# A sparse attention layer as a three-stage pipeline, with float32 up-projections and moved output weights

## The chip, the cores and the metric

The kernel runs on one core of a Trainium2 chip, as one program. The metric is the device time of one execution in microseconds; the table below gives the median of three. TensorE multiplies matrices, VectorE and ScalarE work elementwise on SBUF and PSUM, GpSimd (POOL in the profile) works on SBUF alone, SyncE (SP) issues most of the loads.

## The reference

256 tokens of width 1024 in float32 go through: a sparse attention layer, a feed-forward layer (width 2816), a gated scan layer, a second feed-forward layer, and a block of two mixers with a third feed-forward layer. The change is mainly in the attention layer:

```python
h = x @ w_in                      # 1024 -> 256 (c_q) + 128 (k) + 128 (v) + 128 (k_idx) + 8 (w_idx)
c_q = rms_norm(c_q, g_cq)
q = (c_q @ w_uq)                  # 256 -> 16 heads x 64
q_idx = (c_q @ w_iq)              # 256 -> 8 heads x 128
k_idx = layer_norm(k_idx, g_ik, b_ik)
# rope on q, k, q_idx, k_idx
score = einsum('bqh,bhqs->bqs', w_idx, relu(q_idx . k_idx))   # causal
_, sel = lax.top_k(score, 64)     # 64 keys for each query
p = softmax(q . k[sel] / 8)       # 2 key-value groups of 8 heads
out = (p @ v[sel]) @ w_o          # 1024 -> 1024
h = layer_norm(ALPHA * h + out)
```

The other layers are touched only where they take the root of a variance or mean square, and where the scan layer's constants are loaded.

## The kernel before, in words

The 256 tokens are two row tiles t = 0, 1 of 128 rows. Every weight matrix is streamed: `unit` (L183) loads up to 128x1024 elements into a `raw` tile (four buffers) from SP's queue, and `halves` (L173) makes two reduced float32 tiles of it, the high half `rhi` on ScalarE (L174) and the rest `rlo` on VectorE (L176) or, for the keys in `ON_POOL`, in pieces of 256 columns on GpSimd (L181). `rhi` and `rlo` have nine buffers each. `mm3` (L208) multiplies with three matmuls (L210 to L212), so a product is as good as float32.

The order of the attention layer is the string `DSA` (L1268), whose steps are written one after the other: x turns the input (`newT`), w loads weights, A and B are the input projections, r and f the angle tables, s.t.n the scores of half n of the indexer heads (`score`, L480), q.t.n the queries (`query`, L518), p the top-k (`pick`, L504: eight rounds of maximum and replacement), a.t.g the attention of head group g (`attend`, L523), o.n.t half n of the output projection (L579), n the layer norm, z the transposition for the next layer. Both s and q call `up` (L471): a projection from 256 to 512 columns, a copy to SBUF, `rope` (L369, three elementwise instructions on 128x128) and four transpositions.

The text order is a priority. A planner at build time puts the instructions of each engine into an order by its own estimate of when their inputs are there; on the chip each engine then takes its instructions in that order. `later` (L107) binds the instructions traced within it behind the last one traced so far on VectorE, ScalarE and TensorE.

In `attend` a block is 512 columns of logits: four heads for t = 0 (four blocks in all) and two heads for t = 1 (eight). It multiplies the mask by a large negative diagonal (L534), adds the logits by native float32 matmuls (L538), and calls `softmaxT` (L592): maximum, exponentials and their sums on ScalarE (L599), reciprocal, scaling on ScalarE (L228), four transpositions and a copy on VectorE (L224); then the values (L547). The next block is traced after that. The output weights `dsa_o` are in `ON_POOL`; they are loaded and split where o first asks for them, at the end of the string, but their instructions depend on nothing else.

Roots are taken on GpSimd: `rstd` (L254) scales and adds epsilon (L257) and raises to -0.5 (L258); `rstd_halves` (L891) takes two such additions (L897, L898) and the power (L899). `hgrn_consts` (L696), traced beside the first feed-forward layer, loads three constant blocks into `raw` tiles.

Of the kernel before, what the change touches and what calls it, by code (L numbers as in the profile page):

```python
# [19 lines left out]
P = 128  # L20
D = 1024
# [66 lines left out]
class Net:  # L88
# [6 lines left out]
    def __init__(self, tc, ins, consts, out, ctx):  # L95
# [8 lines left out]
        self.carried = None  # L104

    @contextlib.contextmanager
    def later(self):  # L107
# [5 lines left out]
        engines = {self.nc.vector.engine, self.nc.scalar.engine, self.nc.tensor.engine}  # L113
# [155 lines left out]
    def sumsq(self, s, src, dst, junk):  # L269
        self.nc.scalar.activation(junk[:, : src.shape[-1]], src, AF.Square, accum_out=dst)  # L270

    def ln_residual(self, t, ys, g, b):
# [6 lines left out]
        r = self.rstd(t, mv[:, 1:2], 1, 1.0, LN_EPS)  # L279
# [8 lines left out]
    def norm_heads(self, s, o, heads, d, dst):  # L288
# [3 lines left out]
        nc.scalar.activation(sq, o, AF.Square)  # L292
        ss = self.sm(s, heads, name="ss")
        nc.vector.tensor_reduce(ss, sq, AX.X, ALU.add)
        r = self.rstd(s, ss, heads, 1.0 / d, RMS_EPS)
# [89 lines left out]
    def setup(self):  # L385
# [4 lines left out]
        a = self.bank("y1")  # L390
        for i in range(WARM):
            nc.tensor.matmul(a, warm[:, 0:P], warm[:, 512:1024], start=i == 0, stop=i == WARM - 1)
# [28 lines left out]
    def dsa(self, dst):  # L421
# [8 lines left out]
        w = {}  # L430
# [4 lines left out]
        def inA(t):  # L435
# [4 lines left out]
            self.sumsq(t, a[:, :256], ss, n)  # L440
            r = self.rstd(t, ss, 1, 1.0 / 256, RMS_EPS)
# [14 lines left out]
        def inB(t):  # L456
# [3 lines left out]
            r = self.rstd(t, mv[:, 1:2], 1, 1.0, LN_EPS)  # L460
# [62 lines left out]
        def attend(t, g):  # L523
# [6 lines left out]
            if True:  # L530
                oT = self.bank("dO%d" % t, (P, 4, P), name="oT")
                for i, h0 in enumerate(range(0, 8, per)):
                    L = self.bank("dL%d" % t, (P, per, nk), name="L")
                    nc.tensor.matmul(  # L534
                        L, self.negI, nsel[:, None, :nk].to_broadcast([P, per, nk]), start=True, stop=False
                    )
                    for j in range(0, per, 2):
                        nc.tensor.matmul(  # L538
                            L[:, j : j + 2, :], qT[t][:, g * 4 + (h0 + j) // 2, :], kT[:, g, :, :nk],
                            start=False, stop=j == per - 2,  # L540
                        )
                    pT = self.softmaxT(t, L, per, nk, "d%d" % (i % 2))
                    for j in range(per):
                        h = h0 + j
                        e = (h % 2) * 64
                        for kc in range(t + 1):
                            nc.tensor.matmul(  # L547
                                oT[e : e + 64, h // 2, :], vs[kc][:, g * 64 : (g + 1) * 64],
                                pT[:, j * (t + 1) + kc, :], start=kc == 0, stop=kc == t,
                            )  # L550
                b = slice(g * 4, g * 4 + 4)
                self.halves(OT[t][0][:, b, :], OT[t][1][:, b, :], oT)

        def load(key):
# [6 lines left out]
            else:  # L561
                w[key] = self.group({"iq": w_iq, "uq": w_uq}[key], 0, 1024, 256, "dsa_" + key)
# [4 lines left out]
        def angles(s):  # L567
# [7 lines left out]
            "w": load, "x": turned, "r": angles, "f": lambda: w["r"](), "A": inA, "B": inB, "s": score, "p": pick, "q": query, "a": attend,  # L575
# [3 lines left out]
        def out(n, t):  # L579
            if not rows:  # L580
                rows.extend(self.ln_rows(0, 0))
            if n not in groups:
                groups[n] = self.group(w_o, n * 512, 512, D, "dsa_o")
# [7 lines left out]

    def softmaxT(self, s, L, per, nk, site):  # L592

# [7 lines left out]
        for j in range(per):  # L601
            self.scaled(p[:, j, :], p[:, j, :], rc[:, j : j + 1], "p" + site)
        pT = self.w2(s, (P, 4, P), name="pT")
        self.copy(pT, self.blocksT(self.cols(p.rearrange("p h k -> p (h k)"), 0, 4), site[0] + "P%d" % s), "pT" + site)
        return pT


    def ffn(self, i, HT, wg, wu, wd, finish, turn=None, aside=None):
# [41 lines left out]
        def beside(i):  # L650
            with self.later():
                aside[i]()
# [43 lines left out]
    def hgrn_consts(self):  # L696

        nc, ins, mx = self.nc, self.ins, self.bound
        raw = lambda: self.tile("raw", (P, 1024), F32, "raw")
        sel = self.load(raw()[0:8, :], self.const("sel", 8)).rearrange("p (a b) -> p a b", a=8)  # L700
# [8 lines left out]
        nc.vector.tensor_copy(lev, self.load(raw(), self.const("lev")))  # L709
        msk = self.w1(1, (P, 6, 32), mybir.dt.uint8, name="msk")  # L710
        o, n = OFF["msk"]
        both = self.load(raw()[:, : n + P + 64], self.consts[:, o : o + n + P + 64])
# [178 lines left out]
    def rstd_halves(self, t, halves):  # L891

        nc = self.nc
        s2, v, r = self.sm(t, 2, name="s2"), self.sm(t, 2, name="rv"), self.sm(t, 1, name="rs")
# [490 lines left out]
```

## Time and profile before

| | us |
|---|---|
| median of 3 runs | 1159.03 |
| lowest, highest | 1153.61, 1160.45 |
| profiled execution | 1154.16 |
| its span, first to last instruction | 1152.4 |
| TensorE busy in the span | 1106.6 (96%) |
| VectorE, ScalarE, GpSimd busy | 697.3, 583.9, 224.3 |

A profile is one execution. Busy time of TensorE is modelled to the end of each matmul, so two matmuls in a row overlap by some 0.15 us in the listing; the distance of their starts is what a matmul costs in a row of them. In a listing a row has start, duration, engine, line, operation, out<-in, count, and in brackets the idle time before it and what ended that. The attention layer ends near 120 us.

### The profile page before, as it was taken

To read this page: it belongs to the slowest core of one execution; us is meant where nothing else is said; L and a number is where in the kernel's file an instruction comes from. 1 tells how busy PE (TensorE), PEld (TensorE's weight loads), DVE (VectorE), ACT (ScalarE), POOL (GpSimd) and SP (SyncE) were. 2 spreads that over 40 slices of the span, in tenths; PEclk is the share of its full clock that TensorE was granted. 3 is DMA by queue.
4 is the path that set the end of the run, shared out by engine and by line. 5 is a ranking of instruction groups with operands and counts; after the bars stand their busy time and mean duration, and the time that the engine had idled before them with its cause. 6 is when DMAs were issued, how large, how long until landed. Compare 5 with 4: busy or idle time off the path is not lost.

```text
span 1152.4 us, 15343 instructions
## 1 busy us (share of the span) xinstructions
PE 1106.6 (96%) x5724; PEld 903.0 (78%) x5724; DVE 697.3 (61%) x1061; ACT 583.9 (51%) x832; POOL 224.3 (19%) x336
## 2 busy tenths in 40 slices
PE   8779999999999999999999999999999999999997
PEld 6546888878888777788888887887788878888886
DVE  6986755535566677875545486446655547454542
ACT  5656455525467466444444346763546456453441
POOL 2800620000432223200000022534100181000000
PEclk9989999999999899999999999999999999999999
DMA  8420756547445342365656545663554446566541
GB/s 250 159 85 5 243 166 229 182 119 255 146 146 173 103 145 77 119 214 180 218 183 192 175 131 174 207 159 102 164 192 146 146 146 225 174 222 202 171 140 37
DMA packets 98458, 187.33 MB, mean 163 GB/s; under 512 B 9400, under 2 KB 26952, under 8 KB 98384
## 3 DMA queue, kind: packets, MB, share of 16 engines
q1 hardware_dynamic: 94816, 176.28, 48.1%
q0 software_dynamic: 2864, 9.45, 2.5%
q8 instruction: 45, 0.74, 0.3%
q10 hardware_dynamic: 704, 0.62, 0.2%
q14 instruction: 29, 0.24, 0.1%
HBM read 185.28 MB, written 1.05 MB: 162 GB/s over the span
## 4 chain that ended last, share of the span: by engine, by line
PE 81%; DVE 8%; POOL 4%; DMA 3%; issue 2%; ACT 2%; SPq 0%; POOLq 0%; DVEq 0%; ACTq 0%
PE a L210 15%; PE a L211 15%; PE a L212 15%; PE y L211 8%; PE y L210 8%; PE y L212 8%; PE t L236 3%; POOL rlo L181 2%; DVE rlo L176 1%; PE lv L830 1%; DMA raw<-in_ffn_w_up_dram 1%; DMA raw<-in_ffn_w_gate_dram 1%; DVE m L381 1%; ACT rhi L174 1%; PE L L538 1%
## 5 line engine op out<-in xcount | busy, mean ns | idle before, releaser
L176 DVE TENSOR_TENSOR rlo<-raw,rhi 128x1024 fp32r<-128x1024 f32 (+4 forms) x306 | 370.2, 1215 | 216.3 <-ACT rhi L174 204.8
L174 ACT ACTIVATE rhi<-raw 128x1024 fp32r<-128x1024 f32 (+3 forms) x338 | 352.7, 1047 | 242.8 <-PE y L212 75.5
L210 PE MATMUL a<-rhi,xh 128*128 128x512 f32 (+4 forms) x840 | 318.6, 379 | 3.4 <-ACT sil L625 1.8
L211 PE MATMUL a<-rlo,xh 128*128 128x512 f32 (+4 forms) x840 | 316.7, 377 | 0.2 <-DVE rlo L176 0.2
L212 PE MATMUL a<-rhi,xl 128*128 128x512 f32 (+4 forms) x840 | 315.4, 376 | 0.0
L210 PEld LDWEIGHTS a<-rhi,xh 128*128 128x128 f32 x840 | 158.7, 189 | 32.1 <-ACT xh L174 2.0
L211 PEld LDWEIGHTS a<-rlo,xh 128*128 128x128 f32 x840 | 158.8, 189 | 27.8 <-DVE rlo L176 0.6
L212 PEld LDWEIGHTS a<-rhi,xl 128*128 128x128 f32 x840 | 158.8, 189 | 27.4
L181 POOL TENSOR_TENSOR rlo<-raw,rhi 128x256 fp32r<-128x256 f32 x128 | 99.2, 811 | 179.8 <-ACT rhi L174 179.7
L210 PE MATMUL y<-rhi,hth 128*128 128x512 f32 x264 | 104.7, 396 | 0.5 <-ACT hth L174 0.5
L212 PE MATMUL y<-rhi,htl 128*128 128x512 f32 x264 | 103.2, 391 | 0.0
L211 PE MATMUL y<-rlo,hth 128*128 128x512 f32 x264 | 102.9, 390 | 0.0
L210 PE MATMUL y<-rhi,xh 128*128 128x512 f32 (+2 forms) x152 | 59.1, 390 | 3.1 <-ACT rhi L174 3.1
L257 POOL TENSOR_SCALAR rv<-mv 128x1 f32<-128x1 f32 x10 | 7.2, 716 | 272.0 <-DVE mv L266 271.8
L211 PE MATMUL y<-rlo,xh 128*128 128x512 f32 (+2 forms) x152 | 59.0, 388 | 1.0 <-POOL rlo L181 0.6
L212 PE MATMUL y<-rhi,xl 128*128 128x512 f32 (+2 forms) x152 | 58.6, 387 | 0.0
L174 ACT ACTIVATE hth<-t 128x512 fp32r<-128x512 f32 (+1 forms) x36 | 20.1, 558 | 75.6 <-PE t L236 75.6
L210 PEld LDWEIGHTS y<-rhi,hth 128*128 128x128 f32 x264 | 49.6, 188 | 10.7 <-ACT hth L174 1.1
L212 PEld LDWEIGHTS y<-rhi,htl 128*128 128x128 f32 x264 | 49.5, 188 | 10.6
L211 PEld LDWEIGHTS y<-rlo,hth 128*128 128x128 f32 x264 | 49.6, 188 | 9.7
L631 DVE TENSOR_TENSOR sil<-a,sil 128x512 f32<-128x512 f32 (+1 forms) x36 | 23.2, 643 | 51.1 <-PE a L212 51.0
L625 ACT ACTIVATE sil<-a 128x512 f32<-128x512 f32 (+1 forms) x36 | 20.2, 561 | 58.9 <-PE a L212 58.8
(412 smaller groups left out, 1435.0 us busy)
## 6 DMA issues: line engine op xcount, KB each, us to landing
raw<-in_ffn_w_gate_dram SPq DMA_DIRECT2D x44, 512.0 KB, 4.7
raw<-in_ffn_w_up_dram SPq DMA_DIRECT2D x44, 512.0 KB, 4.7
raw<-in_ffn_w_down_dram SPq DMA_DIRECT2D x44, 512.0 KB, 4.6
raw<-in_hgrn_w_in_dram SPq DMA_DIRECT2D x32, 512.0 KB, 4.5
raw<-in_w_in_dram SPq DMA_DIRECT2D x24, 512.0 KB, 4.4
raw<-in_w_ffn_gate_dram SPq DMA_DIRECT2D x22, 512.0 KB, 4.3
raw<-in_w_ffn_up_dram SPq DMA_DIRECT2D x22, 512.0 KB, 4.6
raw<-in_w_ffn_down_dram SPq DMA_DIRECT2D x22, 512.0 KB, 4.5
```

The lines of the kernel that those rows point to most:

```text
L174: self.nc.scalar.activation(hi, src, AF.Copy)
L176: self.nc.vector.tensor_sub(lo, src, hi.bitcast(F32))
L181: eng.tensor_sub(lo[:, c], src[:, c], hi[:, c].bitcast(F32))
L210: mm(out, xh, wh, start=start, stop=False)
L211: mm(out, xh, wl, start=False, stop=False)
L212: mm(out, xl, wh, start=False, stop=stop)
L236: self.nc.tensor.transpose(tp[:, j, :], b, self.ident)
L381: e2.tensor_tensor(m2, v[:, :, ::-1, :], s[:, None, :, :].to_broadcast(sh), ALU.mult)
L538: nc.tensor.matmul(L[:, j : j + 2, :], qT[t][:, g * 4 + (h0 + j) // 2, :], kT[:, g, :, :nk], start=False, stop=j == per - 2,)
L625: nc.scalar.activation(sil[ci, t][:, :cn], a[:, :cn], AF.Silu)
L631: nc.vector.tensor_mul(sil[ci, t][:, :cn], a[:, :cn], sil[ci, t][:, :cn])
L830: nc.tensor.matmul(lv[64 * c : 64 * c + 64, l - l0, j, :32], y, late, start=True, stop=True)
```

## The change

It does six things.

1. The up-projections use native float32 matmuls: `whole` loads a 128x1024 block of `w_iq` or `w_uq` straight into an `rhi` or `rlo` buffer, `proj4` multiplies once, and `c_q` is no longer split.
2. The attention is a pipeline of three stages, `flow`: with the logits and softmax of one block the transpositions of the block before and the values of the one before that are traced. The mask matmul comes last in a block.
3. The output weights are loaded in two steps `wo.0` and `wo.1`; their ScalarE and GpSimd instructions are bound behind the last ones traced so far, and the first step puts one small GpSimd copy ahead that reads the last roped tile.
4. The order string is another one: queries and scores of both row tiles come ahead of the first attention step.
5. The roots have their scale folded into the square, their epsilon added on VectorE, and one GpSimd instruction left; two places in the attention keep the old form (`rstd_aside`).
6. Thirteen dummy matmuls stand after the second input tile's transposition, and the scan constants are loaded into tiles of the `w4` pool.

```diff
-    def later(self):
+    def later(self, *engines):
...
-        engines = {self.nc.vector.engine, self.nc.scalar.engine, self.nc.tensor.engine}
+        engines = {e.engine for e in engines}
...
+    def whole(self, w, K):
+        res = []
+        for k in range(K // P):
+            raw = self.tile(("rhi", "rlo")[k % 2], (P, 1024), F32, "whole")
+            self.nc.sync.dma_start(raw, w[k * P : (k + 1) * P, :])
+            res.append(raw)
+        return res
+
+    def proj4(self, out, xT, grp, sl):
+        n = len(grp)
+        for k, w in enumerate(grp):
+            self.nc.tensor.matmul(out, xT[:, k, :], w[:, sl], start=k == 0, stop=k == n - 1)
...
-    def rstd(self, s, src, n, scale, eps):
+    def rstd_aside(self, s, src, n, scale, eps):
         v = self.sm(s, n, name="rv")
+        self.nc.gpsimd.tensor_scalar(v, src, scale, eps, ALU.mult, ALU.add)
+        return self.root(s, v, n)
+
+    def root(self, s, v, n):
         r = self.sm(s, n, name="rs")
-        self.nc.gpsimd.tensor_scalar(v, src, scale, eps, ALU.mult, ALU.add)
         self.nc.gpsimd.tensor_tensor(r, v, self.nhalf[:, :n], ALU.pow)
         return r
+
+    def rstd(self, s, src, n, eps):
+        self.nc.vector.tensor_scalar(src, src, eps, None, ALU.add)
+        return self.root(s, src, n)
...
-            c = self.xt("cq")
-            cq[t] = (c[:, 0:2, :], c[:, 2:4, :])
-            self.splitT(n, cq[t][0], cq[t][1], 2, T[t])
+            cq[t] = self.tile("xt", (P, 2, P), F32, "cq")
+            nc.scalar.activation(cq[t], self.blocksT(self.cols(n, 0, 2), T[t]), AF.Copy)
...
-            self.proj(a, cq[t], grp, slice(n * 512, (n + 1) * 512))
-            s = self.w2(t, name="up")
+            self.proj4(a, cq[t], grp, slice(n * 512, (n + 1) * 512))
+            s = turned_last[0] = self.w2(t, name="up")
...
+            for i, h0 in enumerate(range(0, 8, per)):
+                self.flow(
+                    lambda h0=h0, i=i: logits(h0, i),
+                    lambda p, i=i: self.probsT(t, p, "d%d" % (i % 2)),
+                    lambda pT, h0=h0: values(h0, pT),
+                )
...
+        def load_out(n):
+            if n == 0:
+                nc.gpsimd.tensor_copy(self.sm(1, 1, name="gate"), turned_last[0][:, 0:1])
+            with self.later(nc.gpsimd, nc.scalar):
+                groups[n] = self.group(w_o, n * 512, 512, D, "dsa_o")
...
+    def flow(self, *stages):
+        if stages:
+            self.under.insert(0, [stages[0](), list(stages[1:])])
+            for block in self.under[1:]:
+                block[0] = block[1].pop(0)(block[0])
+        else:
+            for block in reversed(self.under):
+                while block[1]:
+                    block[0] = block[1].pop(0)(block[0])
+        self.under = [block for block in self.under if block[1]]
...
     def hgrn_consts(self):
-        raw = lambda: self.tile("raw", (P, 1024), F32, "raw")
-        sel = self.load(raw()[0:8, :], self.const("sel", 8)).rearrange("p (a b) -> p a b", a=8)
+        stage = [self.w4(name="stage") for _ in range(3)]
+        sel = self.load(stage[0][0:8, :], self.const("sel", 8)).rearrange("p (a b) -> p a b", a=8)
...
     def rstd_halves(self, t, halves):
-            self.sumsq(t, halves[n], s2[:, n : n + 1], self.w2(t, dt=BF16, name="sq"))
-        nc.gpsimd.tensor_scalar(v[:, 0:1], s2[:, 0:1], 1.0 / D, RMS_EPS, ALU.mult, ALU.add)
-        nc.gpsimd.tensor_scalar(v[:, 1:2], s2[:, 1:2], 1.0 / D, v[:, 0:1], ALU.mult, ALU.add)
-        nc.gpsimd.tensor_tensor(r, v[:, 1:2], self.nhalf[:, :1], ALU.pow)
-        return r
+            self.meansq(halves[n], s2[:, n : n + 1], self.w2(t, dt=BF16, name="sq"), D)
+        nc.vector.tensor_scalar(v, s2[:, 0:1], RMS_EPS, s2[:, 1:2], ALU.add, ALU.add)
+        return self.root(t, v, 1)
...
-WARM = 10
+WARM, WARM_X = 10, 13
...
 DSA = (
-    "x.0 X.1 x.1 w.A w.A2 r.0 f w.iq A.0 w.B B.0 s.0.0 A.1 B.1 w.uq s.1.0 s.0.1 q.1.0 q.0.0 p.0 s.1.1 q.0.1 a.0.0 "
-    "q.1.1 p.1 a.0.1 a.1.0 a.1.1 o.0.0 o.1.0 n.0 o.0.1 z.0 o.1.1 n.1 r.1"
+    "x.0 X.1 x.1 W w.A w.A2 r.0 f w.iq A.0 w.B B.0 s.0.0 A.1 B.1 w.uq s.1.0 s.0.1 s.1.1 q.0.0 q.0.1 q.1.0 p.0 q.1.1 "
+    "a.0.0 wo.0 p.1 a.0.1 a.1.0 wo.1 o.0.0 a.1.1 o.1.0 n.0 F o.0.1 z.0 o.1.1 n.1 r.1"
 )
```

In the order string W is the dummy matmuls and F ends the pipeline, so that the blocks still under way are finished.

## Rows read from the trace of the kernel before

**Rows 1.** Busy time by stretch: stretch, length, PE, PEld, DVE, ACT, POOL, clock, DMA, GB/s.
```profile
10.00:30.00 20.00, 19.18 (x112) 17.88 (x112) 17.32 (x55) 12.41 (x23) 3.89 (x7) 0.91 0.82 263
30.00:62.00 32.00, 21.25 (x108) 15.41 (x107) 30.55 (x74) 20.32 (x32) 25.40 (x36) 0.95 0.53 176
62.00:81.00 19.00, 14.55 (x75) 9.74 (x75) 16.68 (x50) 11.77 (x50) 0.00 (x0) 0.90 0.15 51
81.00:120.00 39.00, 39.00 (x223) 26.74 (x222) 26.36 (x46) 22.67 (x60) 1.31 (x2) 1.00 0.11 29
```

**Rows 2.** What TensorE waited for over the span: us in total, times, longest.
```profile
PE t L236 <- DVE up L382: 5.5, 2, 4.0
PE t L236 <- DVE h L910: 3.3, 3, 1.5
```

**Rows 3.** VectorE's groups from 27 to 62.5 us: count, busy us, mean ns, idle before.
```profile
L381 DVE TENSOR_TENSOR m<-up,sin 128x128 f32<-128x128 f32 x7 | 7.4, 1064 | 0.0
L380 DVE TENSOR_TENSOR m<-up,cos 128x128 f32<-128x128 f32 x7 | 4.0, 577 | 0.0
L499 DVE SCALAR_TENSOR_TENSOR keep<-rl,wi,keep 128x128 f32<-128x128 f32 x7 | 3.7, 532 | 0.5 <-ACT rl L494 0.4
L382 DVE TENSOR_TENSOR up<-m,m 128x128 f32<-128x128 f32 x7 | 3.5, 503 | 0.1
```

**Rows 4.** The order of time on VectorE and GpSimd, 45 to 60 us.
```profile
45.86 0.68 DVE L224 COPY qiT<-t 128x512 f32<-128x512 f32 x1
...
47.45 0.28 DVE L381 TENSOR_TENSOR m<-up,sin 128x128 f32<-128x128 f32 x1
...
54.67 5.54 POOL L181 TENSOR_TENSOR rlo<-raw,rhi 128x256 fp32r<-128x256 f32 x8
54.69 4.94 DVE L381 TENSOR_TENSOR m<-up,sin 128x128 f32<-128x128 f32 x1
```

**Rows 5.** Groups of the weight split, 0 to 170 us.
```profile
L174 ACT ACTIVATE rhi<-raw 128x1024 fp32r<-128x1024 f32 x35 | 37.0, 1059 | 23.6 <-PE a L212 9.8 <-DMA raw<-in_ffn_w_up_dram 4.5 <-PE y L212 4.4
L176 DVE TENSOR_TENSOR rlo<-raw,rhi 128x1024 fp32r<-128x1024 f32 x26 | 31.6, 1222 | 14.8 <-ACT rhi L174 14.0
L181 POOL TENSOR_TENSOR rlo<-raw,rhi 128x256 fp32r<-128x256 f32 x32 | 23.6, 769 | 5.3 <-ACT rhi L174 5.3
```

**Rows 6.** TensorE in the order of time: an up-projection, then a native float32 product.
```profile
31.57 0.40 PE L210 MATMUL y<-rhi,cq 128*128 128x512 f32 x1
31.81 0.40 PE L211 MATMUL y<-rlo,cq 128*128 128x512 f32 x1
...
81.01 1.02 PE L538 MATMUL L<-kT,qT 128*128 128x512 f32 x2
81.87 0.38 PE L236 MATMUL t<-ident,p 128*128 128x128 f32 x2
```

**Rows 7.** TensorE at the start, in the order of time.
```profile
1.73 3.68 PE L392 MATMUL y<-warm 128*128 128x512 bf16 x10 [1.73 <-POOL warm L389]
...
10.22 0.62 PE L210 MATMUL y<-rhi,xh 128*128 128x384 f32 x2 [3.07 <-ACT rhi L174]
```

**Rows 8.** The first logits and the first product of the feed-forward layer.
```profile
63.16 1.91 PE L538 MATMUL L<-kT,qT 128*128 128x256 f32 x4
...
120.06 0.39 PE L210 MATMUL a<-rhi,xh 128*128 128x512 f32 x1
```

**Rows 9.** Loads and TensorE's gaps in the first feed-forward layer, in the order of time.
```profile
234.52 25.61 SPq L188 DMA_DIRECT2D raw<-in_ffn_w_gate_dram  x6
...
242.99 0.74 PE L236 MATMUL t<-ident,sil 128*128 128x128 f32 x4 [2.05 <-DVE sil L631]
...
277.77 0.39 PE L210 MATMUL a<-rhi,xh 128*128 128x256 f32 x1 [1.79 <-ACT sil L625]
```

**Rows 10.** Busy time by stretch around those gaps, columns as in rows 1.
```profile
240.00:245.00 5.00, 2.95 (x13) 2.16 (x12) 2.44 (x3) 1.66 (x2) 0.00 (x0) 0.84 0.28 75
245.00:250.00 5.00, 5.00 (x20) 4.03 (x19) 2.00 (x3) 1.06 (x1) 0.00 (x0) 0.82 0.16 42
```

More of the change, by code (lines that the diff above doesn't have):

```diff
@@ L267, in meanvar, with meansq @@
         return mv
-    def sumsq(self, s, src, dst, junk):
-        self.nc.scalar.activation(junk[:, : src.shape[-1]], src, AF.Square, accum_out=dst)
+    def meansq(self, src, dst, junk, n):
+        self.nc.scalar.activation(junk[:, : src.shape[-1]], src, AF.Square, scale=n ** -0.5, accum_out=dst)
     def ln_residual(self, t, ys, g, b):
@@ L389, in setup, with keep_warm @@
         nc.gpsimd.memset(warm, 0.0)
-        a = self.bank("y1")
-        for i in range(WARM):
-            nc.tensor.matmul(a, warm[:, 0:P], warm[:, 512:1024], start=i == 0, stop=i == WARM - 1)
+        def keep_warm(count):
+            a = self.bank("a")
+            for i in range(count):
+                nc.tensor.matmul(a, warm[:, 0:P], warm[:, 512:1024], start=i == 0, stop=i == count - 1)
+        self.keep_warm = keep_warm
+        keep_warm(WARM)
         self.X = [self.cp.tile([P, D], F32, name=f"x{t}") for t in range(2)]
@@ L529, in attend, with logits @@
                 OT[t] = (self.xt("oh"), self.xt("ol"))
[L530 to L533, printed above, removed]
+            oT = []
+            def logits(h0, i):
+                L = self.bank("dL%d" % t, (P, per, nk), name="L")
+                for j in range(0, per, 2):
                     nc.tensor.matmul(
-                        L, self.negI, nsel[:, None, :nk].to_broadcast([P, per, nk]), start=True, stop=False
-                    )
-                    for j in range(0, per, 2):
+                        L[:, j : j + 2, :], qT[t][:, g * 4 + (h0 + j) // 2, :], kT[:, g, :, :nk],
+                        start=j == 0, stop=False,
+                    )
+                nc.tensor.matmul(
+                    L, self.negI, nsel[:, None, :nk].to_broadcast([P, per, nk]), start=False, stop=True
+                )
+                return self.softmax(t, L, per, nk, "d%d" % (i % 2))
@@ L538, in attend, with values @@
+            def values(h0, pT):
+                if not oT:
+                    oT.append(self.bank("dO%d" % t, (P, 4, P), name="oT"))
+                for j in range(per):
+                    h = h0 + j
+                    e = (h % 2) * 64
+                    for kc in range(t + 1):
                         nc.tensor.matmul(
-                            L[:, j : j + 2, :], qT[t][:, g * 4 + (h0 + j) // 2, :], kT[:, g, :, :nk],
-                            start=False, stop=j == per - 2,
-                        )
@@ L542, in attend @@
[L542 to L550, printed above, removed]
@@ L551, in attend @@
-                b = slice(g * 4, g * 4 + 4)
-                self.halves(OT[t][0][:, b, :], OT[t][1][:, b, :], oT)
+                            oT[0][e : e + 64, h // 2, :], vs[kc][:, g * 64 : (g + 1) * 64],
+                            pT[:, j * (t + 1) + kc, :], start=kc == 0, stop=kc == t,
+                        )
+                if h0 + per == 8:
+                    b = slice(g * 4, g * 4 + 4)
+                    self.halves(OT[t][0][:, b, :], OT[t][1][:, b, :], oT[0])
+            for i, h0 in enumerate(range(0, 8, per)):
[3 more added lines that the diff above has]
+                    lambda pT, h0=h0: values(h0, pT),
+                )
@@ L561, in load @@
             else:
-                w[key] = self.group({"iq": w_iq, "uq": w_uq}[key], 0, 1024, 256, "dsa_" + key)
+                w[key] = self.whole({"iq": w_iq, "uq": w_uq}[key], 256)
+        def load_out(n):
[3 more added lines that the diff above has]
+                groups[n] = self.group(w_o, n * 512, 512, D, "dsa_o")
         def turned(t):
@@ L590, in dsa, with softmax @@
         self.run(DSA, {**steps, "o": out, "n": close, "z": self.turner(dst)})
-    def softmaxT(self, s, L, per, nk, site):
+    def flow(self, *stages):
[8 more added lines that the diff above has]
+        self.under = [block for block in self.under if block[1]]
+    def softmax(self, s, L, per, nk, site):
         nc = self.nc
@@ L605, in softmaxT @@
         return pT
+    def softmaxT(self, s, L, per, nk, site):
+        return self.probsT(s, self.softmax(s, L, per, nk, site), site)
     def ffn(self, i, HT, wg, wu, wd, finish, turn=None, aside=None):
@@ L650, in beside @@
         def beside(i):
-            with self.later():
+            with self.later(nc.vector, nc.scalar, nc.tensor):
                 aside[i]()
```

31 lines of the change are left out of this document (16 added, 15 removed).

## The prediction

> **What bounds the kernel now.** First view: busy time by stretch of the attention layer, which ends at 120 us [rows 1]. Up to 62 us VectorE is the busiest engine (17.3 of 20 us, then 30.6 of 32) while TensorE has gaps (21.3 of 32); from 81 to 120 us TensorE has none (39.0 of 39). So the layer has two halves: one set by VectorE, one by TensorE. Behind it the feed-forward layers keep TensorE full, so what this layer saves stays saved. Second view: what TensorE waited for over the whole span [rows 2]. The longest entry is the transposition of up-projected rows waiting for rope (5.5 us); the 3.3 us for `h` lie at the two layer ends where an RMS norm follows.
>
> Third view: VectorE's groups from 27 to 62 us [rows 3]. Three rope instructions on one 128x128 shape average 1064, 577 and 503 ns. Fourth view, the order of time [rows 4]: the same instruction takes 0.28 us at 47.45, while GpSimd idles, and 4.94 us at 54.69, where it starts 0.02 us behind a GpSimd run that lasts 5.54 us. That run is the low half of the output weights. A copy out of PSUM at 45.86, beside an earlier such run, took 0.68 us, no longer than elsewhere. So VectorE's elementwise work between two SBUF tiles is held up by GpSimd, and this sits on the path.
>
> **The change, part by part.** The sum is made against the profiled execution, 1154.2 us; its span is 1152.4, so 1.8 us lie around it. The median of the runs shown, 1159.0, is 4.9 us above it.
>
> *Output weights moved.* The 32 GpSimd pieces of 769 ns [rows 5] (24.6 us) now start behind the last rope; their 8 conversions on ScalarE follow the softmax work given so far. Rope gets its clean 0.28 us: 7 x (1.064 + 0.577 + 0.503 - 3 x 0.28) = 9.1 us of VectorE time off the path [rows 3, 4]. Score and key-rope instructions gain too; I leave them out as reserve. SP's queue keeps the eight loads in their place but holds the four raw tiles longer: the first feed-forward loads queue behind the second half. They need about the time TensorE spends in the last output projections, so I cost this at nothing; if that cover fails it is the first rival.
>
> *Native float32 up-projections.* Gone are four splits of 128x1024: 4 x 1.059 us of ScalarE and 4 x 1.222 = 4.9 us of VectorE [rows 5]; the VectorE part counts. The price is TensorE's: today six matmuls per projection, 0.24 us apart from 31.57 to 31.81, so 1.4 us; a native 128x512 product shows as two records that hold the engine from 81.01 to 81.87, 0.86 us [rows 6], so two per projection are 1.7 us. Eight projections cost 8 x 0.3 = 2.4 us more, beside VectorE as long as that is the bound. The small splits of `cq` go as well; their gain is under 1 us and not counted.
>
> *Dummy matmuls before the first projection.* TensorE waits 3.07 us before 10.22 and its first 128x384 products come about 0.31 us apart; ten dummies took 3.68 us [rows 7]. Thirteen take up to 4.8 us at that pace, 1.7 us more than the gap. Against that stands a higher clock sooner. Between -1.7 and +2 us; I take 0, since the split weights arrive one by one there and set the pace either way.
>
> *Order and pipeline.* Logits of the first block start at 63.16, the first feed-forward product at 120.06 [rows 8]. New start of the logits, by VectorE: 63.2 - 9.1 - 4.9, plus what now comes ahead of it (one rope 0.84, four score additions at about 0.53 [rows 3]: 3.0), gives 52. By TensorE: 10.2 plus the busy time of 10 to 62 us, 19.2 + 21.3, gives 50.7, plus seven of the eight dearer projections, 2.1: 53 with no idle at all, less what its first products ran at a lowered clock (mean 0.91 over 20 us [rows 1], so 1.8 us): 51. I take 52. From there to the feed-forward start: TensorE owes 14.6 + 39.0 = 53.6 us [rows 1], so 105.6. ScalarE owes 11.8 + 22.7 = 34.4 us [rows 1] and 8 x 1.06 = 8.5 for the output weights, and needs some 2.5 us before its first exponential; that is 97.4, and then the second half of one projection and one whole one, (12 + 24) x 0.24 = 8.6 [rows 6], so 106.0. Both engines allow 106 against 120: **14 us** saved. Today each block waits for its own softmax, transposition and copy; the three stages let TensorE take the logits of the next block meanwhile, which is what makes 53.6 us of work fit in 54. Without that overlap, 5 us of gaps as today between 62 and 81 (19 - 14.6 [rows 1]) come back: 9 us saved. With the reserve above and a clean pipeline: 20. The mask matmul placed last lets the logits begin before the top-k has ended: worth about 1 us, inside this.
>
> *Scan constants in their own tiles.* SP's queue needs 25.6 us for six gate loads from 234.5, because three of four raw tiles hold constants; TensorE then waits 2.05 and 1.79 us [rows 9] and runs at a mean clock of 0.84 and 0.82 of full for 10 us [rows 10], which is 5 x (0.16 + 0.18) = 1.7 us lost. Together 5.5 us; the new tiles come from a pool that the attention layer has left. I take **5**; bounds 0 (no tile free in time) and 5.5.
>
> *Norm roots.* One GpSimd instruction of each root becomes a VectorE one or goes. Most of these chains lie beside matmuls of the other row tile. What TensorE shows of them is the 3.3 us for `h` [rows 2]; the chain keeps its power on GpSimd, so I take **2**, between -0.5 (VectorE places its short instruction behind a long one) and 4.
>
> Sum: 14 + 5 + 2 = 21, so 1154.2 - 21 = 1133 for the profiled execution. Since that run was low among the three, I set the median 2 us higher: **1135 us**. What is late next is TensorE itself, over almost all of the span.
>
> **A rule against a row.** The copy at 45.86 shows no delay beside GpSimd [rows 4]. The Trainium skill (SBUF — State Buffer, section "Who interferes with whom") says that VectorE and GpSimd share one port pair under an exclusive lock, taken by two-SBUF-input instructions and by copies in a two-port mode. By its first half the moved GpSimd work finds only the one mask comparison per row tile to block, so the sum stands; by its second half the twelve probability copies would be exposed, and that is the slower rival below. For a source in PSUM the row speaks for the first.
>
> **Rivals.**
> 1. *The gain is given back in the attention.* The second half of the output weights may convert only behind the first group's softmax of row tile 1; its four units need 1.06 + 4 x 4 x 0.77 = 13.4 us [rows 5], and 24 products (24 x 0.24 = 5.8 us) of row tile 1 follow. If that softmax ends at 92 instead of about 80, the feed-forward starts at 92 + 13.4 + 6 x 0.24 + 5.8 = 113, or its own weights are late by as much. For it: GpSimd's and SP's queues are in order. Against: ScalarE had 7 us of idle time in the 19 from 62 to 81 [rows 1], so the softmax can come sooner. Attention saves 7 instead of 14, with the rest 14: 1142 (median scale).
> 2. *The constants don't help*, because the stream there is slow for another reason or the new tiles come free late. For it: six loads spread over 25.6 us [rows 9] would also fit a slow memory. Against: the feed-forward layers before and after run the same stream with TensorE full. 1140.
> 3. *Slower: the hold-up travels with GpSimd's work.* Place: the twelve blocks' reductions and copies and the top-k of row tile 1, which now run beside the 24.6 us on GpSimd. Price: a hold like that at 54.69, 4.94 us [rows 4], once per unit, on six of the eight: 29.6 us. The feed-forward would start at 106 + 29.6 = 136, 16 later than now; less 7 from the other parts, and 2 for the scale: 1165. It decides from 21 us of such holds. Against it is the copy at 45.86; in the rows only instructions with two SBUF inputs suffer.
>
> **How the numbers follow.** Forecast 0.62 (its own range 1127 to 1141), first rival 0.18, second 0.12, third 0.05, the rest for a gain above the forecast's range. A measurement of this kernel can tell about 1% from no change, here 1147.4. The first rival reaches beyond that with about a third of its weight (the pipeline failing too), the second with a small part: faster 0.83, same 0.12, slower 0.05. The range takes in every bound of the parts on the good side, 1154 - 20 - 5.5 - 4 = 1124.5, and rivals 1 and 2 together, 1147, on the other: 1124 to 1149.
>
> **What would show it.** Right: rope on 128x128 near 0.28 us each; first logits near 52 us; first feed-forward product near 106; GpSimd's pieces all behind the last rope; no TensorE wait between 234 and 280 us and the clock full there; the native products as two records of 0.43 us. Wrong: feed-forward product after 112 us with TensorE idle between 60 and 100 (rival 1); SP still taking 25 us for six loads (rival 2); VectorE instructions of several microseconds beside GpSimd in the attention (rival 3). If TensorE is full from 12 us on and the layer still ends late, the native products were too dear.

## The result: 0.6% faster, and the attention layer no sooner done

| | before | changed |
|---|---|---|
| median of 14 runs each, side by side, us | 1154.31 | 1147.62 |
| ratio, 95% interval | | 0.9941 (0.9919 to 0.9964) |
| span of the profiled execution, us | 1152.4 | 1147.8 |
| first logits, us | 63.16 | 53.90 |
| first feed-forward product, us | 120.06 | 122.88 |

The gain is 6.7 us where 21 were forecast, and less than the 1% that the prediction took as the bound of what can be told from no change. The logits come 9.3 us sooner, as forecast within 2 us, and the attention layer ends 2.8 us later. What was gained was gained behind it. TensorE in the changed kernel, in order of time: a native projection, the first logits, the first mask, a later wait, the first feed-forward product (columns as in [rows 6]; here and below, L is a line of the kernel that was run, so the numbers differ from those of the kernel before).

```profile
49.13 1.88 PE L222 MATMUL y<-whole,cq 128*128 128x512 f32 x4
...
53.90 1.46 PE L565 MATMUL L<-kT,qT 128*128 128x256 f32 x6
...
58.28 0.59 PE L569 MATMUL L<-keep,negI 128*128 128x512 bf16 x2 [1.78 <-DVE keep L546]
...
102.81 0.67 PE L581 MATMUL oT<-pT,keep 128*64 128x128 f32 x8 [2.66 <-DVE pT L240]
...
122.88 0.39 PE L226 MATMUL a<-rhi,xh 128*128 128x512 f32 x1
```

The same stretch by busy time answers to [rows 1] (first 30 to 54 us, then from the first logits on):

```profile
30.00:54.00 24.00, 23.77 (x110) 14.71 (x109) 16.93 (x62) 10.38 (x19) 1.31 (x3) 1.00 0.06 22
...
53.90:58.00 4.10, 2.52 (x14) 1.74 (x13) 4.05 (x22) 2.68 (x4) 0.73 (x2) 1.00 0.20 52
58.00:76.00 18.00, 12.64 (x44) 6.56 (x44) 10.70 (x32) 13.76 (x50) 7.53 (x11) 0.72 0.19 55
76.00:99.80 23.80, 23.80 (x138) 14.94 (x136) 14.00 (x25) 18.77 (x52) 13.26 (x21) 1.00 0.36 108
99.80:108.00 8.20, 5.54 (x25) 4.18 (x24) 4.38 (x6) 2.72 (x8) 1.27 (x2) 0.79 0.60 188
108.00:122.88 14.88, 14.88 (x81) 11.64 (x81) 13.40 (x19) 7.39 (x9) 1.00 (x1) 1.00 0.33 92
```

Read PE (third figure) and the clock (eighth, the counts in brackets left aside) together. From 30 to 54 us TensorE is idle for 0.2 us and VectorE for 7.1: TensorE has become the bound there. After the logits, busy time times clock is an estimate of work done: 2.5 + 9.1 + 23.8 + 4.4 + 14.9 = 54.7 us of work in 69.0 us. So 14.3 us are lost, 8.9 of them from 58 to 76 and 3.8 from 99.8 to 108. The same estimate for the kernel before gives 52.3 us of work in 56.9, so 4.6 lost.

The first loss lies ahead of the first output product. The output projection begins with `oh`, the attended rows of the first head group, which ScalarE copies out of PSUM (`oT`). Before, then changed:

```profile
75.81 0.60 ACT L174 ACTIVATE oh<-oT 128x512 fp32r<-128x512 f32 x1 [0.56 <-PE oT L547]
76.45 0.50 PE L210 MATMUL y<-rhi,oh 128*128 128x512 f32 x1 [0.70 <-ACT oh L174]
```

```profile
67.35 3.88 ACT L175 ACTIVATE rhi<-raw 128x1024 fp32r<-128x1024 f32 x4
...
70.85 0.66 PE L581 MATMUL oT<-pT,keep 128*64 128x128 f32 x8
...
75.41 0.59 ACT L175 ACTIVATE oh<-oT 128x512 fp32r<-128x512 f32 x1
...
76.56 0.59 PE L226 MATMUL y<-rhi,oh 128*128 128x512 f32 x1
```

The first output product comes at 76.56 us, as late as before (76.45), though the logits began 9.3 us sooner: that lead is all used up here. Before, `oh` was copied 0.05 us behind its last product; now it is copied 3.9 us behind it (75.41 against 71.51), when ScalarE has done the exponentials of the third and fourth blocks, and four conversions of output weights stand ahead of those. From the first output product to the feed-forward layer it takes 46.3 us instead of 43.6.

The second loss lies in that last stretch and comes from VectorE and GpSimd (answers to [rows 4]):

```profile
90.01 11.06 POOL L182 TENSOR_TENSOR rlo<-raw,rhi 128x256 fp32r<-128x256 f32 x16 [10.54 <-ACT rhi L175]
...
97.79 4.36 DVE L177 TENSOR_TENSOR rlo<-raw,rhi 128x1024 fp32r<-128x1024 f32 x1
```

The low half of a feed-forward weight, 1.22 us elsewhere, takes 4.36 beside GpSimd's second run; the copy `pT` behind it is what TensorE waits for until 102.81. The hold of [rows 4] has moved from rope to here.

In the first feed-forward layer the gaps of [rows 9] and the lower clock of [rows 10] are gone,

```profile
230.00:280.00 50.00, 50.00 (x254) 42.18 (x253) 25.09 (x26) 24.24 (x28) 0.00 (x0) 1.00 0.55 180
```

and the waits for `h` in [rows 2] fall from 3.3 to 1.8 us:

```profile
PE t L252 <- DVE h L977: 1.8, 3, 0.7
```

### The profile page after: what moved, and what is told of

It is laid out like the page before. It is cut to its first block, busy times and chain, and to the rows that moved or that the text cites. A ratio compares the mean times of both kernels' runs of the same rounds, so it can differ in the third digit from the quotient of the medians.

```text
span 1147.8 us, 15285 instructions
## 1 busy us (share of the span) xinstructions
PE 1114.7 (97%) x5721; PEld 902.3 (79%) x5721; DVE 686.3 (60%) x1083; ACT 580.5 (51%) x828; POOL 204.4 (18%) x301
## 5 line engine op out<-in xcount | busy, mean ns | idle before, releaser
L175 ACT ACTIVATE rhi<-raw 128x1024 fp32r<-128x1024 f32 (+4 forms) x334 | 347.9, 1047 | 230.1 <-PE y L228 79.6
L278 POOL TENSOR_TENSOR rs<-mv,nhalf 128x1 f32<-128x1 f32 x8 | 8.0, 996 | 241.8 <-DVE mv L283 241.8
```

Source lines behind the costliest of these rows:

```text
L175: self.nc.scalar.activation(hi, src, AF.Copy)
```

## The experiments

Each profile starts a little differently (the first projection at 9.7 to 11.5 us), so "layer" below is the time from the first projection's product to the first feed-forward product. The three kernels with the attention layer of before show its scatter: 109.8, 111.9 and 109.5 us. "Hold" is the longest VectorE instruction that was held up beside GpSimd from 27 to 122 us; "output" is the first output product.

| run | first logits | output | hold | layer | ratio to before, 95% interval |
|---|---|---|---|---|---|
| before | 63.16 | 76.45 | 4.94 rope | 109.8 |  |
| changed | 53.90 | 76.56 | 4.36 | 112.3 | 0.9941 (0.9919 to 0.9964) |
| e1 constants and roots alone | 65.11 | 78.41 | 4.94 rope | 111.9 | 0.9944 (0.9926 to 0.9962) |
| e12 constants alone | 63.42 | 76.72 | 4.96 rope | 109.5 | 0.9975 (0.9961 to 0.9990) |
| e2 second half's low parts on VectorE | 53.76 | 77.34 | none | 109.4 | 0.9941 (0.9916 to 0.9966) |
| e3 top-k early | 53.69 | 75.51 | 1.62 | 108.0 | 0.9918 (0.9893 to 0.9943) |
| e4 ScalarE untied | 53.68 | 77.00 | none | 107.0 | 0.9922 (0.9897 to 0.9947) |
| e5 both | 54.14 | 80.31 | 4.47 mask | 110.9 | 0.9947 (0.9929 to 0.9964) |
| e7 no pipeline | 53.53 | 73.52 | 2.71 | 119.8 | one run, 1158.71 us |
| e8 no ties | 65.45 | 88.78 | under 1.5 | 118.0 | one run, 1155.59 us |
| e16 no dummies | 54.94 | 78.02 | 1.60 | 108.5 | 0.9919 (0.9891 to 0.9947) |
| e6 projections split | 49.91 | 72.54 | 1.60 | 103.7 | one run, 1142.18 us |
| e9 the same, timed | 49.14 | 71.49 | 4.37 | 106.3 | 0.9890 (0.9868 to 0.9911) |
| e10 the same again | 49.18 | 71.51 | 4.36 | 106.5 | one run, 1139.45 us |
| e11 = e9 + e2 | 49.52 | 72.74 | none | 104.3 | 0.9861 (0.9839 to 0.9883) |
| e13 = e11 + e3 | 49.36 | 73.36 | none | 106.2 | 0.9887 (0.9858 to 0.9915) |
| e14 all low parts on VectorE | 57.62 | 80.28 | none | 114.0 | 0.9946 (0.9925 to 0.9967) |
| e15 = e11 + matmuls in the gap | 49.54 | 72.62 | none | 105.8 | 0.9876 (0.9844 to 0.9907) |
| e17 = e11 + e4 | 50.20 | 78.80 | 1.52 | 109.5 | 0.9917 (0.9886 to 0.9947) |
| e18 = e11, output weights later | 49.50 | 73.14 | none | 108.6 | 0.9911 (0.9875 to 0.9946) |

From the first output product to the feed-forward layer the pipelined kernels take 40.6 to 43.8 us where no hold of over 4 us falls into that stretch (e18 45.4), and 44.7 to 46.3 where one does (changed, e9, e10); e7 takes 56.9.

**e1 and e12: what is not attention.** e1 is the kernel before with the change's scan constants and norm roots, e12 with the constants alone:

```diff
-        raw = lambda: self.tile("raw", (P, 1024), F32, "raw")
+        stage = [self.w4(name="stage") for _ in range(3)]
```

> The kernel before with two parts of the change alone: the scan constants in tiles of their own and the new norm roots; its attention layer is untouched. Theory: the changed kernel's attention layer costs 2.8 us (first feed-forward product at 122.88 us against 120.06) and the constants bring 6.5 in the first feed-forward layer, so here the first feed-forward product stands at 120 as before, the waits of 2.05 and 1.79 us are gone, and the whole is some 2.8 us faster than the changed kernel: ratio to before about 0.992. Rival: the later gain hangs on how the new attention leaves SP's queue; then the constants alone bring little, ratio 0.997 or above.

> The kernel before with the scan constants in tiles of their own and nothing else. From the first feed-forward product to the first sigmoid of the scan layer the kernel before takes 202.7 us, the changed one 196.2 and the kernel of e1 197.9. Theory (the constants alone do it): 196 to 198 here, the transpositions of h at the ends of the layers still wait up to 1.5 us as before, ratio to before 0.995 to 0.996, e1's 0.9944 plus 1 to 2 us for the roots. Rival (the roots are worth nothing): ratio as e1, 0.994.

Without any change of the attention layer e1 reaches 0.9944, the ratio of the whole change. So the new attention layer as it stands is worth nothing that can be measured. My expectation of 0.992 for e1 was wrong: the 2.8 us by which the changed layer ends later are no more than the scatter of a layer that is left alone (e1's own took 111.9 us). The constants alone are worth 0.25%, 2.9 us (from the first feed-forward product to the scan layer's first sigmoid 198.5 us against 202.7), less than the 0.4 to 0.5% that I expected; the roots are the rest, 0.31% or 3.6 us, with intervals that just touch.

**e2 to e5: the hold and the start of the softmax.** The edits of e2, e3 and e4 in this order, long lines cut to what changes; e5 has the last two:

```diff
-                groups[n] = self.group(w_o, n * 512, 512, D, "dsa_o")
+                groups[n] = self.group(w_o, n * 512, 512, D, "dsa_o%d" % n)
-    "b2_g0", "b2_kn", "b2_vm", "b2_w_out", "dsa_o", "h_d",
+    "b2_g0", "b2_kn", "b2_vm", "b2_w_out", "dsa_o0", "h_d",
...
-s.1.1 q.0.0 q.0.1 q.1.0 p.0 q.1.1
+p.0 s.1.1 q.0.0 q.0.1 q.1.0 q.1.1
...
-            with self.later(nc.gpsimd, nc.scalar):
+            with self.later(nc.gpsimd):
```

> The changed kernel, but the low halves of the second half of the output weights are computed on VectorE, so GpSimd is idle after 80 us. Theory (the hold travelled): the feed-forward split at 97.79 that took 4.36 us takes 1.2, TensorE's wait of 2.66 us before 102.81 and the half clock behind it go; four splits of 1.22 on VectorE find room there (7.4 of 10 us busy from 90 to 100). First feed-forward product at 119 to 120 instead of 122.9, whole time 3 to 4 us under the changed kernel, ratio 0.991. Rival (the native products made TensorE the bound): no change, 0.994. Rival (VectorE becomes the bound): later, 0.996.

> The changed kernel with one step moved: the top-k of row tile 0 is asked for before the last index scores and the query projections of row tile 1. Theory: the first softmax was late because its mask waits for the top-k (1.78 us before 58.28) and its reciprocal stands behind top-k rounds of row tile 1 (scale waits 1.93 us before 62.84); with the mask there earlier the first exponentials start at 57 or before instead of 59.41 and the half clock from 60 to 70 shrinks: first feed-forward product 1 to 3 us earlier, ratio 0.991 to 0.993. Rival (ScalarE's own work between 59 and 76 sets the pace, or TensorE is the bound): the exponentials start earlier but the feed-forward product moves by under 0.5 us, 0.994.

> The changed kernel without the tie on ScalarE: the eight conversions of the output weights may run between the softmax blocks one by one, the low halves on GpSimd stay tied behind the last rope. Theory: the four conversions in a row at 67.35 (3.88 us) and 88.89 (3.88 us) kept the exponentials waiting and let GpSimd start 13 us after its gate at 55.44; untied, both halves end some 10 us sooner, the second before the feed-forward split of 97.79, which then takes 1.2 us instead of 4.36: first feed-forward product 2 to 5 us earlier, ratio 0.990 to 0.992. Rival (the hold only moves to another VectorE instruction with two SBUF inputs): a hold of 3 to 5 us is seen elsewhere, and the product stays at 122 to 123, 0.994.

> The changed kernel with both edits that helped: the top-k of row tile 0 asked for earlier, and no tie on ScalarE. Theory (two separate losses, one at the start of the softmax, one from the late output weights): the gains of 5.0 us (117.84 against 122.88) and 4.7 us (118.21) add up in part, the first feed-forward product stands at 114 to 116, ratio to before 0.988 to 0.991. Rival (both only move the same softmax chain): 117 to 118, ratio 0.992.

Where no hold is left (e2, e4) the layer is 3 to 5 us shorter in the profile; the times alone do not separate e2 from the changed kernel (0.9941 both, where I expected 0.991), and e3's and e4's intervals overlap with its own. e5 should have been the best and is not. VectorE and GpSimd in e5:

```profile
63.68 8.92 POOL L182 TENSOR_TENSOR rlo<-raw,rhi 128x256 fp32r<-128x256 f32 x13
...
68.41 4.47 DVE L546 TENSOR_TENSOR keep<-work,keep 128x256 bf16<-128x256 f32 x1
```

The hold fell on the mask comparison of row tile 1, the very instruction that the prediction named as the only one to block; the mask matmul waited 2.68 us for it. In e5 VectorE's instruction ends 0.28 us behind GpSimd's run (72.88 against 72.60), in the changed kernel 1.1 us behind it (102.15 against 101.07). That is about what each takes alone (0.42 and 1.22 us elsewhere), so both look to have waited until the run was over. Not every such instruction does: rope's in [rows 4] ended at 59.63, 0.58 us before GpSimd's run, and in e8, beside a GpSimd run of 11.73 us, rope instructions on 128x128 took at most 0.81 us.

The Trainium skill (SBUF — State Buffer, "Who interferes with whom") says that a VectorE instruction with two SBUF inputs contends with a GpSimd instruction that reads SBUF, and that whoever issues first keeps the shared ports for the whole instruction. As to which instructions are held the traces agree; these holds span several GpSimd instructions, 4.36 and 4.47 us against pieces of 0.69 (11.06 us for 16).

**e7 and e8: pipeline and ties.** e7 runs all stages of a block at once, e8 drops the gate and `later`.

> The changed kernel with each attention block given in one piece: logits, softmax, transposition and values at once, as before. Theory (the pipeline works where the softmax chain keeps up, from 78 us on): TensorE shows waits in 76 to 105 us of 3 us or more in all and the first feed-forward product is 2 to 6 us later than 122.88. Rival (the three-stage order is what makes TensorE wait for ScalarE at the start, since logits of the next block stand ahead of finished work): the same or earlier, 120 to 123.

> The changed kernel without the gate and without the ties: the output weights are converted when their data and the engines allow, as before. Theory (rope is held up beside GpSimd): a rope instruction of 4 to 5 us is seen again between 30 and 56 us, first logits 2 to 9 us later than 53.9; but no hold at 97, so the feed-forward product at 119 to 124. Rival (the ties cost more than they bring): logits within 1 us of 53.9 and the product at 117 or before.

Without the pipeline the layer is 7.5 us longer, with waits of TensorE for `pT` (3.3 us in all) and for the low halves (3.1). But ahead of the first output product e7 is the quicker one: there `oh` is copied 0.05 us behind its last product, and the output projection starts 3.0 us sooner. Without the ties the logits start at 65.45 and the feed-forward product comes at 129.37, both later than I expected. TensorE's longest wait is for the key's rope (4.3 us), yet no single instruction takes 4 us, so that part of the expectation was wrong: the root of the key's norm stands on GpSimd among the pieces of the output weights (VectorE waits 2.61 us for it), and rope instructions beside GpSimd take up to 0.81 us. The ties are needed, then, but not only for the reason that the prediction gave; the rest of the 11.5 us is not explained.

**e6, e9, e10: the native products undone.**

```diff
-            self.proj4(a, cq[t], grp, slice(n * 512, (n + 1) * 512))
+            self.proj(a, cq[t], grp, slice(n * 512, (n + 1) * 512))
```

> The changed kernel with the up-projections in split form as before (six products per projection from hi and lo halves, four splits of 128x1024 on ScalarE and VectorE). Theory (VectorE is the bound up to 54 us, a native projection costs 1.72 us against 1.44): first logits 2 to 5 us later than 53.9, first feed-forward product 1 to 4 us later than 122.88. Rival (the native products made TensorE the bound from 30 to 54 us, where it shows no gap): logits 1 to 2 us earlier, feed-forward product 120 to 121.

> The kernel of e6 again, timed in rounds: its profile had the first feed-forward product at 114.51 us against 122.88 with native products. If the native products cost the attention layer those 8.4 us, the ratio to before is 0.986 to 0.989 against 0.994 with them. Rival (the profile of e6 was a good start of one execution, as starts of the first product differ by 2 us between profiles): 0.990 to 0.994.

> The kernel of e9 a second time, for one more profile: how far the first feed-forward product moves between two executions of one kernel. Start noise alone: 113 to 116 us. Rival (the hold in the feed-forward split comes and goes with the alignment of GpSimd's pieces): the split near 94 us takes 1.6 us in one and 4 in the other.

(e10 is e9's kernel, in spite of its name.) TensorE, then its busy time from 30 to 50 us, in e6:

```profile
49.22 0.39 PE L226 MATMUL y<-rhi,cq 128*128 128x512 f32 x1
49.45 0.39 PE L227 MATMUL y<-rlo,cq 128*128 128x512 f32 x1
...
30.00:50.00 20.00, 19.93 (x111) 15.84 (x111) 16.83 (x70) 10.44 (x20) 1.58 (x4) 1.00 0.21 79
```

Three matmuls 0.23 us apart cost 0.69 us where a native pair costs 0.86. TensorE is full with either form, so what is saved on it shortens the layer: logits 4.0 us sooner in e6, the layer 6.0 shorter at the same hold (e9 against the changed kernel). The ratios' intervals do not touch: part 1 of the change cost it 0.5%. Sixteen native pairs at 0.17 us more than three matmuls explain 2.7 us of that; the rest was not taken apart. The rival that I had set against my own theory in e6 is the one that holds, with two to four times the size that I gave it. The hold itself differs between executions of one kernel (1.60, 4.37 and 4.36 us): in e6 VectorE's split got in behind one piece, at 93.75, and GpSimd's run took 12.05 us instead of 11.07.

**e11: the best.** e9 with the edit of e2.

> Up-projections split again, and the low halves of the second half of the output weights on VectorE, so that no GpSimd run stands beside the feed-forward split near 94 us. That split took 1.60 us in e6, so there is 0.4 us of hold to win and four splits of 1.2 us to pay on VectorE, which has room: first feed-forward product at 113 to 115, ratio within 0.002 of e9. Rival (the hold is worth the 2.8 us that it was worth with native products): 111 to 112.

0.9861 is 1.4% under the kernel before, and its interval is wholly under that of the changed kernel. Against e9 it is 0.3%, with overlapping intervals; the profiles say 2 us.

**e13 to e18: what the start of the softmax still loses.** e11 does some 8 us of work in the 18.1 from 53.4 to 71.5 us:

```profile
53.40:71.50 18.10, 14.59 (x44) 7.90 (x44) 11.82 (x36) 14.90 (x50) 7.73 (x12) 0.56 0.21 71
```

Each run takes one supposed cause away: the late top-k (e13, the edit of e3), GpSimd and the tied conversions (e14: no `dsa_o` in `ON_POOL`, with the edits of e3 and e4), the clock (e15), the tied conversions alone (e17, the edit of e4; e18, `wo.0` behind `a.0.1`). e16 is the changed kernel with `WARM_X = 0`. For e15 (`JUNKS = 8`):

```diff
+                if t == 0 and g == 0:
+                    junk = self.bank("y0", (P, per, nk), name="junk")
+                    for r in range(JUNKS):
+                        nc.tensor.matmul(
+                            junk, self.negI, nsel[:, None, :nk].to_broadcast([P, per, nk]), start=r == 0, stop=r == JUNKS - 1
+                        )
```

> The kernel of e11 with the top-k of row tile 0 asked for earlier, as in e3. With native products that moved the first feed-forward product by 5 us (117.84 against 122.88), part of it by another alignment of the hold (1.62 against 4.36 us). Theory (the mask and the reciprocals set the start of the softmax): first exponentials 1 to 2 us earlier than 54.85, first feed-forward product 2 to 3 us earlier than 115.5, ratio 0.984 against 0.986. Rival (e3 gained by the alignment of the hold alone): first product within 1 us of e11, ratio 0.986.

> The kernel of e13 with no low half on GpSimd and no tie on ScalarE: VectorE computes all eight low halves of the output weights, ScalarE converts them where it has room, most of them before the first softmax. Theory (the run of four conversions, 3.88 us, keeps the exponentials waiting): 66.82 for the third block's exponentials in e6 becomes 63, first feed-forward product 2 to 4 us earlier than in e13, ratio 0.981 to 0.983. Rival (VectorE, 9.4 of 10 us busy from 40 to 50 us, is the bound there and pays 4.9 us for the first four): logits 2 to 5 us later, first product no earlier than in e13, ratio 0.985 to 0.989.

> The kernel of e11 with eight matmuls without a use (128x512, the mask once more, into another PSUM bank) behind the mask of each of the first two blocks. TensorE runs at half clock in part of 57 to 72 us there (0.67 mean from 60 to 70 in e6). Theory (the half clock itself costs the start of the softmax 2 to 3 us, because logits and transpositions take twice as long): the clock stays full from 56 to 65, first feed-forward product 1 to 3 us earlier than e11, ratio 0.984. Rival (ScalarE and VectorE set the pace there, the clock is only a sign of the waiting): the clock is full and the first product does not move, or moves later by up to the 2 to 3 us that the sixteen matmuls take, ratio 0.986 to 0.988.

> The changed kernel without the thirteen dummy matmuls before the first projection. The changed kernel's first products start at 10.54 us with a full clock from 10 to 20 us, the kernel before started at 10.22 with 0.83. Theory (weights arrive one by one and set the pace there): first logits within 0.5 us of 53.9, ratio 0.994. Rival (the half clock of the first products is lost time that nothing hides): logits 1 to 2 us later, ratio 0.995 to 0.996.

> The kernel of e11 without the tie on ScalarE: its conversions of the output weights run one by one between the softmax blocks instead of four in a row; the first half's low parts stay on GpSimd behind the last rope, the second half's on VectorE. Theory (the first 18 us of the attention are set by ScalarE's softmax of row tile 0 and the conversions among it): exponentials of the third block at 64 to 65 instead of 66, first output projection 2 to 4 us earlier than in e11 (72.74), first feed-forward product 1 to 3 us earlier, ratio 0.983 to 0.985. Rival (total ScalarE work counts, not its order): no change, 0.986. Rival (GpSimd now starts at the gate and holds up a VectorE instruction of the top-k's end, as in e5 4.47 us): 2 to 3 us later, 0.988.

> The kernel of e11 with the first half of the output weights asked for behind the attention of both groups of row tile 0, so that ScalarE's four conversions stand behind the exponentials of the fourth block instead of between the second and the third. Theory: exponentials of the third block at 62 to 63 instead of 66, row tile 0 attended 3 to 4 us sooner, but the output weights 4 to 8 us later; if the start of the softmax is what counts, TensorE works ahead on row tile 1 and the first feed-forward product is 1 to 3 us earlier, ratio 0.984. Rival (the output projections are TensorE's only long work and must not wait for their weights): a new wait for the low halves of 2 us or more, first product 0 to 4 us later, ratio 0.986 to 0.990.

None makes the layer shorter than e11's; e14's and e17's intervals lie wholly above its own. In e13 the mask was ready 0.9 us sooner than in e11, but the first exponentials came 1.2 us later (56.04 against 54.85), so it does not clear the top-k of blame. What e3 had gained lies for the most part behind the first output product (42.3 us from there instead of 46.3), where its hold is short. e15 has a higher clock in the stretch and no gain:

```profile
53.40:71.50 18.10, 13.89 (x60) 7.43 (x60) 12.00 (x38) 14.94 (x51) 8.00 (x12) 0.86 0.25 77
```

ScalarE's 14.9 of 18.1 us are the same as in e11, so the half clock is a sign of the waiting there, not its cause. In e14 the output weights are split among the up-projections, and the logits start at 57.62, later than either expectation. In e17 the mask came late instead (TensorE waits 2.50 us for it). In e18, with the conversions behind the fourth block, `oh` follows the first exponentials by 13.3 us instead of e11's 15.9, but TensorE then waits for GpSimd's pieces as the output projection begins. In all sixteen profiles of pipelined kernels `oh` is copied where the exponentials of the fourth block end, within 0.02 us, and 1.7 to 6.4 us behind its last product; no run moved that copy alone. e16: from first projection to first logits 43.4 us with and without the dummies; its logits are 1.0 us later because the first projection was, within the range of starts.

## Why the prediction was wrong

- **The engine sums ("Both engines allow 106 against 120").** This step failed. TensorE's owed work was nearly right (53.6 us of busy time forecast, 54.7 of work by the estimate above), the start nearly so (52 and 53.90), but 14.3 us were lost between, against 4.6 before. TensorE's long work, the output projections, can only start with `oh`, and each block comes to that through VectorE, ScalarE and VectorE again; two sums of engine totals cannot see such a chain. It took 22.7 us from the first logits to the first output product, where it had taken 13.3. The traces show three things in it: the mask, whose comparison starts 4.0 us behind the first logits (0.7 us ahead of them before), four conversions on ScalarE (3.88 us), and `oh` 3.9 us behind its last product. What each costs the layer stays open: moving the conversions gave nothing (e14, e17, e18), e13 did not bring the exponentials forward, a higher clock gave nothing, and `oh` was not tried.
- **The overlap ("the three stages let TensorE take the logits of the next block meanwhile").** Right behind the first output product, where e7 loses most; wrong ahead of it, where e7 starts that product 3.0 us sooner.
- **Native products ("beside VectorE as long as that is the bound").** The price of one was right (1.72 us), the cover was not. Once rope is freed, TensorE is full from 30 us on, and the products lie on the path: the 2.4 us that were costed at nothing measure 2.7 by the rows, and undoing the whole part shortened the layer by 6.0. Against that stood the 4.9 us of VectorE's splits counted as gain, for an engine that was no longer the bound.
- **The hold ("finds only the one mask comparison per row tile to block, so the sum stands").** Wrong in what it overlooked: the feed-forward split has two SBUF inputs too, and runs beside GpSimd's second half. It costs one hold of 4.36 us (in some executions 1.6) and 2 to 3 us of the layer, not the 29.6 us of rival 3. On the comparison it was right, as e5 shows.
- **Rope's relief** came as forecast: rope at 0.27 to 0.29 us, logits 9.3 us sooner where 11 were forecast. The pipeline is worth 7.5 us of the layer (5 forecast) in e7's one profile. Both were spent on the two losses above.
- **Constants 5, roots 2:** 2.9 and 3.6 us by the times. Their sum, 6.5 against 7, is the whole gain; that it fits is in part luck, since the two misses cancel. Dummies 0: right.
- **Rivals.** The first had the right place, the attention layer, and its sign came (a feed-forward product after 112 us, TensorE idle between 60 and 100), but its mechanism was wrong: GpSimd's second half ended at 101.07, TensorE was not kept waiting for it. The second did not come: SP needs 18.48 us for the six loads instead of 25.61 and TensorE has no gap from 230 to 280. The third came in small. The sign named last in the prediction, a full TensorE and a late end, is what the trace shows from 30 to 54 us.

## What to carry to other kernels

When a change relieves the bound of a stretch, price its other parts against the engine that is the bound afterwards. Add up an engine's owed work only over stretches in which that work can start; where the long work waits for a chain, the chain sets the time. In a software pipeline, look at where the last step of a finished group stands in the order of the engine that does it. When a block of GpSimd work is moved, list every VectorE instruction with two SBUF inputs in its new neighbourhood, those of the next layer's prefetch too.

## What was not expected of the hardware

Two executions of e9's kernel (e9 and e10) agree within 0.04 us at the landmarks from 49 to 380 us, with the same wait of TensorE at 382 (0.67 us), and then differ in the clock. 385 to 390 us in e9, then in e10:

```profile
385.00:390.00 5.00, 5.00 (x29) 3.91 (x28) 2.30 (x8) 2.67 (x4) 0.00 (x0) 0.50 0.00 0
```

```profile
385.00:390.00 5.00, 5.00 (x34) 3.92 (x33) 4.12 (x9) 3.65 (x5) 1.57 (x2) 1.00 0.06 5
```

One runs at the lower level (1.2 GHz), the other at the full one, and ends 2.9 us sooner at the next landmark, the transpositions of `h` (660.92 against 663.79 us). The profiles of before and of the changed kernel both have the drop, e1 and e11 do not. One profile of this kernel can so be 3 us off another without any cause in the program.

The hold is as little fixed. In six profiles the same feed-forward split starts 0.20 to 0.22 us behind the start of a GpSimd piece, with four more to come. In three (changed, e9, e10) it took 4.36 to 4.37 us, in three (e3, e6, e16) 1.60 to 1.62. Nothing in the profile tells the two apart beforehand.
